# A hybrid decoder layer: parity of the weight buffers, x scaled and rounded in one instruction, half-group splits and two load queues at the start

## The chip, the cores and the metric

The kernel runs on one core of one Trainium2 chip. A core has five engines that run side by side: PE (TensorE, the matrix multiplier), DVE (VectorE), ACT (ScalarE), POOL (GpSimd) and SP (SyncE, which here only issues transfers). Sixteen DMA engines carry data between HBM and the on-chip memory. The metric is the device time in microseconds (us); lower is better.

## The reference

One layer with SEQ = 256 rows and D_MODEL = 2048 is computed in float32: a half-step of a gated feed-forward net (SwiGLU, width 5632), a mixer of attention and gated linear attention, a cross-attention, and a second feed-forward half-step.

```python
x = x + 0.5 * swiglu(rms_norm(x, ffn1_norm[l]), ffn1_w_gate[l], ffn1_w_up[l], ffn1_w_down[l])
x = x + hybrid_mixer(rms_norm(x, mix_norm[l]), pos, w_in[l], ...)
x = x + cross_attention(rms_norm(x, xattn_norm[l]), rms_norm(mem, mem_norm[l]), ...)
x = x + 0.5 * swiglu(rms_norm(x, ffn2_norm[l]), ffn2_w_gate[l], ffn2_w_up[l], ffn2_w_down[l])

def swiglu(h, w_gate, w_up, w_down):
    return (jax.nn.silu(h @ w_gate) * (h @ w_up)) @ w_down
```

The gain of a norm multiplies the columns of x before the product; the factor of each row (the reciprocal root of its mean square) is applied behind it, to the result. So the products of the first half-step need only x times gain.

## The kernel before, in words

**Products.** A weight matrix comes in groups: 512 rows of the inner dimension (four slices k of 128) by 512 columns, 1 MB in float32. PE multiplies in a rounded 32-bit form, so each operand is split into a rounded high part and the remainder: ACT writes the high part (`wh`, line 136), DVE subtracts it from the original for the low part (`wl`, line 137; `split`). A product is then three matmuls, high by high, low by high, and high by low (`mm3`, lines 163 to 165). The rows of x stand on the two sides of a tile t (2 x 128 rows), so a group is 4 x 2 x 3 = 24 matmuls. x itself is held transposed and split in the same way (`xTh`, `xTl`, one pair for each 512 columns). `proj` runs one block of 512 columns over its four groups. From the second block of a half-step on, gate and up are made together by a Strassen-like scheme (`strassen`), which needs the sums `fa`, `fb`, `sa`, `sb` of parts of x (`sums_of`, lines 177 to 186); these are made while the first up block runs.

**Buffers.** The loaded float32 group (`raw`) goes to one of two rings of three buffers: `wp`, which lives for the whole kernel, and `FRAW`, which belongs to the pool of a phase (`half1`, `middle`, `half2`). In the two half-steps `load` (line 121) takes the rings in turn: odd loads of a phase go to `FRAW`, even ones to `wp`; in the middle phase all go to `wp`. The pool of `half2` takes the memory of the pool of `middle`, so a first use of its buffers waits until the tiles that lay there have been read. The split parts `wh` and `wl` have rings of three (`ws`).

**Start.** Three groups of the first gate block and three quarters of x are loaded ahead of all else, x and weights in turn, on SP's queue (lines 108 to 117): the first group in slices of k, the other two in halves. Then `first` (line 432) scales x by the gain and splits it: in slices for group 0 (ACT scales in place at line 295, ACT rounds at line 298, DVE subtracts at line 299), and in halves on POOL (line 297), ACT and DVE for the other three groups. Only group 0 is split slice by slice (`fine` in `wgroup`); groups 1 to 3 are split in one piece. Ten matmuls on a constant run on PE before the first real one (line 428).

**Order.** A scheduler orders the instructions of each engine by priorities and by its own simulation of when operands and buffers come free; `later`/`tick` delay some steps by a count of half groups. Each engine then runs its list strictly in order. SP issues loads in one list too: a load that waits for its buffer holds up all loads behind it, and each hardware DMA also waits for the one eight DMAs earlier, since there are eight DMA semaphores.

**Second half-step.** It begins when the cross-attention's output projection is done: x is updated (line 936), its squares are summed (line 304), and `norm_chunk` transposes it on PE (line 315), scales it by the gain (DVE, line 317) and splits it (lines 320 and 321), one column chunk of 512 after the other. Then `proj` takes the first gate block of `ffn2`.

Of the kernel before, what the change touches and what calls it, by code (L numbers as in the profile page):

```python
# [16 lines left out]
P = 128  # L17
# [31 lines left out]
def layer_kernel(ctx: ExitStack, tc: tile.TileContext, A: dict, out: bass.AP):  # L49
# [24 lines left out]
    def FT(tag, bufs, shape, dt, name):  # L74
        return phase["pool"].tile(shape, dt, tag=tag, name=name, bufs=bufs)
# [31 lines left out]
    with tc.high_priority(100000):  # L107
        SY.dma_start(gain, A["gains"])
        for g in range(3):
            raw = wp.tile([P, 4, 512], F32, tag="raw", name="raw")  # L110
            wload.append(raw)
            step = 2 if g else 1
            xr = FT("h", 8, [P, 4, S], F32, "xr")
            xload.append(xr)
            for k in range(0, 4, step):
                SY.dma_start(xr[:, k:k + step], A["xT"][g, :, k:k + step])
                SY.dma_start(raw[:, k:k + step], A["ffn1_w_gate"][0, g, :, k:k + step])
    xs = [con.tile([P, TT, 512], F32, name=f"x{c}") for c in range(NC)]


    def load(W, c, g):

        if wload:
            return wload.pop(0)
        kn, n = W.shape[-2:]
        with tc.high_priority(WPRI):
            phase["loads"] += 1
            if phase["half_step"] and phase["loads"] % 2:
                raw = FT("raw", FRAW, [P, kn, n], F32, "raw")
            else:  # L130
                raw = wp.tile([P, kn, n], F32, tag="raw", name="raw")
            SY.dma_start(raw, W[c, g])
        return raw

    def split(wh, wl, src):
        SC.copy(wh, src)  # L136
        V.tensor_sub(wl, src, wh.bitcast(F32))  # L137

    def split_tiles(kn, n):
        return tuple(ws.tile([P, kn, n], F32R, tag=x, name=x) for x in ("wh", "wl"))  # L140
# [1 line left out]
    def wgroup(W, c, g, fine=None):  # L142

        raw = load(W, c, g)
        n = W.shape[-1]
        kn = W.shape[-2]
        with tc.high_priority(WPRI):
            wh, wl = split_tiles(kn, n)
            for i in range(kn if fine else 1):
                d = slice(i, i + 1) if fine else slice(0, kn)  # L150
                if fine:
                    fine(i)
                split(wh[:, d], wl[:, d], raw[:, d])
        ks = [(kn * g + kk, wh[:, kk], wl[:, kk]) for kk in range(kn)]
        yield ks[:kn // 2]
        yield ks[kn // 2:]
# [98 lines left out]
    def proj(W, c, lhs, groups, fine=None, last=False):  # L255

        n = W.shape[-1]
        acc = [pa.tile([P, n], F32, tag="acc", name="acc") for _ in range(TT)]
        groups = list(groups)
        for i, g in enumerate(groups):  # L260
            if fine and i:
                fine(4 * i)
            if last and i == len(groups) - 1:
                both = [w for half in wgroup(W, c, g) for w in half]
                for t in range(TT):
                    mm3(acc, lhs, both, i == 0, True, (t,))
                break
            for h, half in enumerate(wgroup(W, c, g, fine if i == 0 else None)):
                mm3(acc, lhs, half, i == 0 and h == 0, i == len(groups) - 1 and h == 1)
                tick()  # L270
        return acc
# [8 lines left out]
    def xtiles(c):  # L280
        hi = con.tile([P, 4, S], F32R, name=f"xTh{c}", tag=f"xTh{c}")
        lo = con.tile([P, 4, S], F32R, name=f"xTl{c}", tag=f"xTl{c}")
        xT[c] = (hi, lo)
        return hi, lo
# [6 lines left out]

    def packed(xr, k0, n, hi, lo, g0):

        if n == 1:
            SC.activation(xr[:, 0], xr[:, 0], AF.Copy, scale=gain[:, g0 + k0:g0 + k0 + 1])
        else:
            G.tensor_tensor(xr, xr, gain[:, g0 + k0:g0 + k0 + n].unsqueeze(2).broadcast_to([P, n, S]), op=ALU.mult)
        SC.copy(hi, xr)
        V.tensor_sub(lo, xr, hi.bitcast(F32))

# [45 lines left out]
    def ffn(pre, r, after, fine=None, last=False):  # L346
# [18 lines left out]
        for part in PARTS:  # L365
            for f in part:
# [11 lines left out]
                        sg.append(s)  # L378
                if sums is None:
                    sums = tuple(FT(n, 1, [P, 4, 4, P], F32R, n) for n in ("sh", "sl"))  # L380
                    sums_of(xT[0], xT[1], lambda i: tuple(p[:, 2 * i:2 * i + 2] for p in sums))
                    upv = proj(wu, f, lhs_x, range(4))
                hs = []
                with tc.high_priority(WPRI):
# [44 lines left out]
    ident = con.tile([P, P], F32, name="ident")  # L429
    make_identity(nc, ident)  # L430

    def first(k):
        if k < 4:
            if k == 0:
                xtiles(0)
            hi, lo = xT[0]
            packed(xload[0][:, k:k + 1], k, 1, hi[:, k:k + 1], lo[:, k:k + 1], 0)
            if k == 3:
                xload.pop(0)
        else:  # L440
            with tc.high_priority(WPRI):
                hi, lo = xtiles(k // 4)
                if xload:
                    xr = xload.pop(0)
                else:
                    xr = FT("h", 8, [P, 4, S], F32, "xr")
                    SY.dma_start(xr, A["xT"][k // 4])
                for j in (0, 2):
                    packed(xr[:, j:j + 2], k + j, 2, hi[:, j:j + 2], lo[:, j:j + 2], 0)

    def load_x():
        ss1 = new_ss("ss1")
# [580 lines left out]
```

## Time and profile before

| | |
|---|---|
| time, median of 3 runs | 1958.72 us (1958.36 to 1960.1) |
| profiled execution, its own time | 1957.67 us |
| its span, first to last instruction | 1955.9 us |
| PE busy | 1925.7 us, 98% |
| DVE busy | 1261.5 us, 64% |
| ACT busy | 976.7 us, 50% |
| POOL busy | 98.1 us, 5% |
| DMA, mean | 213 GB/s |
| mean granted TensorE clock | 0.995 |

All durations that are used below come from this one profiled execution; the time outside its span is 1957.67 - 1955.9 = 1.8 us. In the rows of a timeline the first number is the start in us from the span's start, the second the duration, then come engine, line, operation, the tile written and the tiles read, and in brackets how long the engine had stood idle and what ended that. SPq is SP's queue of DMA issues. Successive matmuls overlap in these rows: each is shown at about 0.39 us, while the starts lie 0.227 us apart.

### The profile page before, as it was taken

The numbers are of one execution on the slowest core, as the hardware profiler recorded it, in microseconds if no ns is written. First come the engines' busy times: TensorE is split into PE (matmuls) and PEld (weight loads), VectorE is DVE, ScalarE is ACT, GpSimd is POOL, SyncE is SP. The second block draws the span as 40 slices with busy tenths as digits, with TensorE's granted clock in tenths as the row PEclk, the third lists the DMA queues.
The fourth block names the chain that finished last, engine by engine and source line by source line (L and its number), as shares of the span: only waits on it lengthen the run. The fifth ranks groups of instructions, "written<-read, shape, count | busy, mean of one in ns | idle before, by whom it ended". The sixth has DMA issues, their size and how long they took to land.

```text
span 1955.9 us, 21245 instructions
## 1 busy us (share of the span) xinstructions
PE 1925.7 (98%) x8760; PEld 1586.1 (81%) x8760; DVE 1261.5 (64%) x947; ACT 976.7 (50%) x876; POOL 98.1 (5%) x101
## 2 busy tenths in 40 slices
PE   8999999999999999999999999899999999999999
PEld 6888878888878888778888889788888788887887
DVE  7776467775578655446775555677746777457863
ACT  6555345553356446444566445545534555335642
POOL 2000000000000000012221000000000000000000
PEclk9999999999999999999999999899999999999999
DMA  9677557775567734445456553567755777556771
GB/s 368 234 236 258 191 146 265 273 267 192 173 222 236 281 127 161 153 169 189 172 215 215 185 182 144 204 228 248 253 193 150 258 271 267 211 177 215 237 284 60
DMA packets 63292, 416.13 MB, mean 213 GB/s; under 512 B 7099, under 2 KB 8251, under 8 KB 14428
## 3 DMA queue, kind: packets, MB, share of 16 engines
q1 hardware_dynamic: 56284, 370.74, 49.6%
q0 software_dynamic: 5760, 41.95, 10.4%
q10 hardware_dynamic: 1152, 2.10, 0.3%
q8 instruction: 68, 1.11, 0.2%
q14 instruction: 28, 0.23, 0.0%
HBM read 370.72 MB, written 2.10 MB: 191 GB/s over the span
## 4 chain that ended last, share of the span: by engine, by line
PE 74%; DVE 16%; ACT 6%; issue 4%; DMA 1%; POOL 0%; SPq 0%; ACTq 0%; DVEq 0%
PE acc L164 20%; PE acc L165 20%; PE acc L163 20%; DVE wl L137 10%; ACT wh L136 5%; PE x L194 5%; DVE raw L212 4%; PE acc L194 1%; PE x L165 1%; PE x L164 1%; PE x L163 1%; DVE h L387 1%; PE y L194 1%; DVE acc L238 1%; PE tp L315 0%
## 5 line engine op out<-in xcount | busy, mean ns | idle before, releaser
L137 DVE TENSOR_TENSOR wl<-raw,wh 128x2048 fp32r<-128x2048 f32 (+1 forms) x407 | 919.2, 2278 | 591.8 <-ACT wh L136 589.9
L136 ACT CAST wh<-raw 128x2048 fp32r<-128x2048 f32 (+1 forms) x407 | 762.4, 1898 | 656.2 <-PE acc L165 477.7
L163 PE MATMUL acc<-wh,xTh 128*128 128x512 f32 x1024 | 403.3, 395 | 15.5 <-ACT wh L136 15.5
L164 PE MATMUL acc<-wl,xTh 128*128 128x512 f32 x1024 | 402.9, 393 | 7.1 <-DVE wl L137 7.0
L165 PE MATMUL acc<-wh,xTl 128*128 128x512 f32 x1024 | 400.7, 391 | 0.0
L163 PE MATMUL acc<-wh,hTh 128*128 128x512 f32 x704 | 274.7, 390 | 0.0
L165 PE MATMUL acc<-wh,hTl 128*128 128x512 f32 x704 | 274.0, 389 | 0.0
L164 PE MATMUL acc<-wl,hTh 128*128 128x512 f32 x704 | 273.9, 389 | 0.0
L163 PEld LDWEIGHTS acc<-wh,xTh 128*128 128x128 f32 x1024 | 193.0, 189 | 59.0 <-ACT wh L136 18.6
L164 PEld LDWEIGHTS acc<-wl,xTh 128*128 128x128 f32 x1024 | 193.5, 189 | 55.4 <-DVE wl L137 16.1
L165 PEld LDWEIGHTS acc<-wh,xTl 128*128 128x128 f32 x1024 | 193.4, 189 | 39.8
L165 PEld LDWEIGHTS acc<-wh,hTl 128*128 128x128 f32 x704 | 132.1, 188 | 27.4
L164 PEld LDWEIGHTS acc<-wl,hTh 128*128 128x128 f32 x704 | 132.2, 188 | 27.3
L163 PEld LDWEIGHTS acc<-wh,hTh 128*128 128x128 f32 x704 | 132.2, 188 | 27.1
L216 POOL DMA_DIRECT2D raw<-raw x40 | 34.6, 865 | 1179.2 <-DVE raw L212 966.2
L212 DVE TENSOR_TENSOR raw<-raw 128x2048 f32<-128x2048 f32 x40 | 91.5, 2287 | 0.7
L165 PE MATMUL x<-wh,xTl 128*128 128x512 f32 x160 | 62.3, 389 | 0.0
L164 PE MATMUL x<-wl,xTh 128*128 128x512 f32 x160 | 62.3, 389 | 0.0
L163 PE MATMUL x<-wh,xTh 128*128 128x512 f32 x160 | 62.2, 389 | 0.0
L228 ACT COPY acc<-x 128x512 f32<-128x512 f32 x20 | 11.4, 571 | 95.6 <-PE x L194 95.6
L163 PE MATMUL acc<-wh,mTh 128*128 128x512 f32 x128 | 50.1, 392 | 0.0
L165 PE MATMUL acc<-wh,mTl 128*128 128x512 f32 x128 | 49.8, 389 | 0.0
(302 smaller groups left out, 1945.0 us busy)
## 6 DMA issues: line engine op xcount, KB each, us to landing
raw<-in_ffn_w_up_dram SPq DMA_DIRECT2D x88, 1024.0 KB, 7.0
raw<-in_ffn_w_down_dram SPq DMA_DIRECT2D x88, 1024.0 KB, 5.0
raw<-in_ffn_w_gate_dram SPq DMA_DIRECT2D x85, 1024.0 KB, 7.1
raw<-in_w_in_dram SPq DMA_DIRECT2D x48, 1024.0 KB, 4.8
raw<-raw POOLq DMA_DIRECT2D x40, 1024.0 KB, 6.9
raw<-in_w_out_dram SPq DMA_DIRECT2D x16, 1024.0 KB, 4.8
raw<-in_xattn_w_k_dram SPq DMA_DIRECT2D x4, 1024.0 KB, 5.6
raw<-in_xattn_w_q_dram SPq DMA_DIRECT2D x4, 1024.0 KB, 4.7
```

Of the source, the lines that this page charges most:

```text
L136: SC.copy(wh, src)
L137: V.tensor_sub(wl, src, wh.bitcast(F32))
L163: PE.matmul(acc[t], lh, wh, start=first and i == 0, stop=False, skip_group_check=seeded)
L164: PE.matmul(acc[t], lh, wl, start=False, stop=False, skip_group_check=seeded)
L165: PE.matmul(acc[t], ll, wh, start=False, stop=last and i == len(half) - 1, skip_group_check=seeded)
L194: PE.matmul(acc, lhs(k)[i], w[:, k], start=first, stop=j == 1 and k == 3, skip_group_check=not start)
L212: V.tensor_add(dst, x, y)
L216: G.dma_start(dst, x, accum_op=ALU.add)
L228: SC.copy(c0l, x)
L238: V.tensor_sub(c0r, ys, x)
L387: V.scalar_tensor_tensor(h, upv[t], r[:, t:t + 1], sg[t], op0=ALU.mult, op1=ALU.mult)
```

## The change

Five edits, all in how work is loaded and split:

1. In the half-steps the even loads of a phase go to `FRAW` and the odd ones to `wp`; before it was the other way round. So the first weight load of a half-step goes to the ring that lives for the whole kernel.
2. In the first gate block x is scaled and rounded in one ACT instruction (`activation` with the gain as scale, straight into `xTh`), and DVE makes the remainder from the unscaled x in one instruction ((x times gain) minus `xTh`), slice by slice for all four groups. POOL takes no part, and no scaled float32 x is written.
3. The groups 1 to 3 of that block are split in halves of two slices, each right behind its half of x.
4. The first two weight slices are loaded on ACT's queue, beside x on SP's.
5. The sums of `sums_of` in a half-step are issued after the last split of the gate block (`issue_after`).

```diff
-                SY.dma_start(raw[:, k:k + step], A["ffn1_w_gate"][0, g, :, k:k + step])
+                (SC if g == 0 and k < 2 else SY).dma_start(raw[:, k:k + step], A["ffn1_w_gate"][0, g, :, k:k + step])
...
-            if phase["half_step"] and phase["loads"] % 2:
+            if phase["half_step"] and phase["loads"] % 2 == 0:
                 raw = FT("raw", FRAW, [P, kn, n], F32, "raw")
...
+    last_split = []
+
     def split(wh, wl, src):
         SC.copy(wh, src)
-        V.tensor_sub(wl, src, wh.bitcast(F32))
+        last_split[:] = [V.tensor_sub(wl, src, wh.bitcast(F32)).ins]
...
-            for i in range(kn if fine else 1):
-                d = slice(i, i + 1) if fine else slice(0, kn)
+            step = fine[0] if fine else kn
+            for i in range(0, kn, step):
+                d = slice(i, i + step)
                 if fine:
-                    fine(i)
+                    fine[1](kn * g + i, step)
                 split(wh[:, d], wl[:, d], raw[:, d])
...
-            if fine and i:
-                fine(4 * i)
...
-            for h, half in enumerate(wgroup(W, c, g, fine if i == 0 else None)):
+            for h, half in enumerate(wgroup(W, c, g, (2 if i else 1, fine) if fine else None)):
...
-        if n == 1:
-            SC.activation(xr[:, 0], xr[:, 0], AF.Copy, scale=gain[:, g0 + k0:g0 + k0 + 1])
-        else:
-            G.tensor_tensor(xr, xr, gain[:, g0 + k0:g0 + k0 + n].unsqueeze(2).broadcast_to([P, n, S]), op=ALU.mult)
+        G.tensor_tensor(xr, xr, gain[:, g0 + k0:g0 + k0 + n].unsqueeze(2).broadcast_to([P, n, S]), op=ALU.mult)
...
-                    sums_of(xT[0], xT[1], lambda i: tuple(p[:, 2 * i:2 * i + 2] for p in sums))
+                    with tc.issue_after(last_split[0]):
+                        sums_of(xT[0], xT[1], lambda i: tuple(p[:, 2 * i:2 * i + 2] for p in sums))
...
+    def first(k0, n):
+        g = k0 // 4
+        if k0 % 4 == 0:
+            xtiles(g)
+            if not xload[g:]:
+                xload.append(FT("h", 8, [P, 4, S], F32, "xr"))
+                SY.dma_start(xload[g], A["xT"][g])
+        hi, lo = xT[g]
+        for k in range(k0, k0 + n):
+            x, h, c = xload[g][:, k % 4], hi[:, k % 4], gain[:, k:k + 1]
+            SC.activation(h, x, AF.Copy, scale=c)
+            V.scalar_tensor_tensor(lo[:, k % 4], x, c, h.bitcast(F32), op0=ALU.mult, op1=ALU.subtract)
```

**ACT at the start of the program.** `xr` is the loaded x, `xTh_132`, `xTh_178`, `xTh_214` and `xTh_250` are the high parts of its four quarters (numbered 132, 176, 216, 258 after the change), `raw` and `wh` the loaded group and its high part. Before, from the last slice of group 0 on:

```order
L295 ACTIVATE xr<-xr,gain 128x256
L298 CAST xTh_132<-xr 128x256
L136 CAST wh<-raw 128x512
L298 CAST xTh_178<-xr 128x512 x2
L136 CAST wh<-raw 128x2048
L298 CAST xTh_214<-xr 128x512 x2
L136 CAST wh<-raw 128x2048 x2
L298 CAST xTh_250<-xr 128x512 x2
```

And after the change, at the same place:

```order
L441 ACTIVATE xTh_132<-xr,gain 128x256
L138 CAST wh<-raw 128x512
L441 ACTIVATE xTh_176<-xr,gain 128x256 x2
L138 CAST wh<-raw 128x1024
L441 ACTIVATE xTh_176<-xr,gain 128x256 x2
L138 CAST wh<-raw 128x1024
L441 ACTIVATE xTh_216<-xr,gain 128x256 x2
L138 CAST wh<-raw 128x1024
L441 ACTIVATE xTh_216<-xr,gain 128x256 x2
L138 CAST wh<-raw 128x1024
L441 ACTIVATE xTh_258<-xr,gain 128x256 x4
L138 CAST wh<-raw 128x1024 x2
```

The first half of a group is now split before the second half of x is touched, and the instructions no longer wait for POOL. DVE's list changes in the same way, and the sums `fa` and `fb` now stand behind the low part of group 3 instead of between groups 2 and 3.

**SP at the start of the second half-step.** The gate groups 0 to 3 of `ffn2` are `raw_8597`, `raw_8667`, `raw_8697`, `raw_8727`; the first up groups are 8779, 8809, 8839, 8869. Before, in the order of issue, with what each load waits for (DMAHW: an earlier DMA; DVE, PE: a reader of the buffer):

```order
L132 DMA raw_8667<-in_ffn2_w_gate_dram 128x2048 [waits DMAHW5_49,DVE_49]
L132 DMA raw_8727<-in_ffn2_w_gate_dram 128x2048 [waits DMAHW6_49,DVE_49]
L132 DMA raw_8809<-in_ffn2_w_up_dram 128x2048 [waits DMAHW7_49,DVE_49]
L132 DMA raw_8597<-in_ffn2_w_gate_dram 128x2048 [waits PE_49]
L132 DMA raw_8697<-in_ffn2_w_gate_dram 128x2048
L132 DMA raw_8779<-in_ffn2_w_up_dram 128x2048
```

After the change the gate groups are `raw_8605`, `raw_8675`, `raw_8705`, `raw_8735`, the up groups 8787, 8817, 8847, 8877:

```order
L132 DMA raw_8605<-in_ffn2_w_gate_dram 128x2048 [waits DMAHW5_49,DVE_49]
L132 DMA raw_8705<-in_ffn2_w_gate_dram 128x2048 [waits DMAHW6_49,DVE_49]
L132 DMA raw_8787<-in_ffn2_w_up_dram 128x2048 [waits DMAHW7_49,DVE_49]
L132 DMA raw_8847<-in_ffn2_w_up_dram 128x2048 [waits DMAHW0_49,DVE_49]
L132 DMA raw_8675<-in_ffn2_w_gate_dram 128x2048 [waits PE_49]
L132 DMA raw_8735<-in_ffn2_w_gate_dram 128x2048
L132 DMA raw_8817<-in_ffn2_w_up_dram 128x2048
```

Group 0 was the fourth load issued and is now the first; groups 1 and 3 are now behind an up group that waits for DVE.

**ACT at the same place.** `junk` are the sums of squares of the four chunks x0 to x3, `xTh0` to `xTh3` the high parts of the transposed chunks. Before:

```order
L304 ACTIVATE junk_8465,ss4_8383<-x1_104 128x512
L304 ACTIVATE junk_8467,ss4_8383<-x1_104 128x512
L320 CAST xTh0_8491<-xg_8498 128x4x128
...
L320 CAST xTh2_8615<-xg_8622 128x4x128
L320 CAST xTh2_8615<-xg_8631 128x4x128
L320 CAST xTh3_8635<-xg_8642 128x4x128
L136 CAST wh_8599<-raw_8597 128x2048
L136 CAST wh_8669<-raw_8667 128x2048
L136 CAST wh_8699<-raw_8697 128x2048
L320 CAST xTh3_8635<-xg_8651 128x4x128
L136 CAST wh_8729<-raw_8727 128x2048
```

After:

```order
L302 ACTIVATE junk_8473,ss4_8391<-x1_104 128x512
L138 CAST wh_8607<-raw_8605 128x2048
L302 ACTIVATE junk_8475,ss4_8391<-x1_104 128x512
L318 CAST xTh0_8499<-xg_8506 128x4x128
...
L318 CAST xTh2_8623<-xg_8630 128x4x128
L318 CAST xTh2_8623<-xg_8639 128x4x128
L138 CAST wh_8677<-raw_8675 128x2048
L138 CAST wh_8707<-raw_8705 128x2048
L138 CAST wh_8737<-raw_8735 128x2048
L318 CAST xTh3_8643<-xg_8650 128x4x128
```

The high part of group 0 has moved ahead of twelve instructions; group 1 now stands where group 0 stood. PE's list follows: the first twelve matmuls of the gate block now stand before the transposes of x2 and x3 (line 315), the other twelve of group 0 behind them, and then group 1. Apart from these places and a few neighbours within the first gate and up blocks of the two half-steps, PE, ACT and DVE keep their order.

More of the change, by code (lines that the diff above doesn't have):

```diff
@@ L430, in layer_kernel @@
     make_identity(nc, ident)
[L432 to L449, printed above, removed]
+    def first(k0, n):
[10 more added lines that the diff above has]
+            V.scalar_tensor_tensor(lo[:, k % 4], x, c, h.bitcast(F32), op0=ALU.mult, op1=ALU.subtract)
     def load_x():
```

## The prediction

> **What bounds the kernel now.** I read the page first (busy shares), then the table of 50 us windows, then PE's waits, then the timeline of the two places that these pointed to.
>
> ```profile
> PE 1925.7 (98%) x8760; PEld 1586.1 (81%) x8760; DVE 1261.5 (64%) x947; ACT 976.7 (50%) x876; POOL 98.1 (5%) x101
> 0.00:50.00 50.00, 42.81 (x172) 33.88 (x173) 34.94 (x30) 31.07 (x42) 9.78 (x15) 0.93 0.94 367
> 250.00:300.00 50.00, 47.56 (x209) 38.64 (x208) 34.56 (x20) 21.73 (x14) 1.70 (x2) 1.00 0.56 172
> 1200.00:1250.00 50.00, 43.38 (x206) 36.14 (x205) 33.35 (x41) 24.83 (x37) 0.70 (x1) 0.90 0.50 189
> 1500.00:1550.00 50.00, 48.48 (x217) 39.53 (x216) 36.63 (x22) 26.44 (x18) 1.71 (x2) 1.00 0.68 223
> PE acc L163 <- ACT wh L136: 15.5, 8, 4.6
> PE acc L164 <- DVE wl L137: 7.0, 17, 2.1
> ```
>
> In a window row the columns behind the length are busy us (and instructions) of PE, PEld, DVE, ACT and POOL, then the granted clock, the DMA share and GB/s. PE is the bound: it lacks 1955.9 - 1925.7 = 30.2 us. Of these 7.2 lie in the first 50 us and 6.6 in 1200 to 1250, where the clock was below 1 as well; the other windows lack 0 to 2.4. The waits name the cause, the two split instructions. So a microsecond saved on PE in one of these two places is saved at the end, as long as no load becomes late behind it.
>
> **Place 1, the start, as it was.**
>
> ```profile
> 13.37 0.39 PE L165 MATMUL acc<-wh,xTl 128*128 128x512 f32 x1
> 16.52 1.22 PE L163 MATMUL acc<-wh,xTh 128*128 128x512 f32 x2 [2.76 <-ACT wh L136]
> 22.85 0.61 PE L163 MATMUL acc<-wh,xTh 128*128 128x512 f32 x1
> 23.28 0.42 PE L164 MATMUL acc<-wl,xTh 128*128 128x512 f32 x1
> 37.36 0.39 PE L163 MATMUL acc<-wh,xTh 128*128 128x512 f32 x1
> 0.00:23.20 23.20, 11.38 (x34) 0.86 0.89 329
> 23.20:37.00 13.80, 13.80 (x62) 1.00 1.03 424
> 18.00:20.00 2.00, 0.30 (x1) 0.30 (x2) 2.00 (x2) 1.95 (x2) 0.00 (x0) 0.50 1.00 416
> ```
>
> Group 0 ends at 13.8; then PE waits for the split of the whole group 1, runs its next matmuls at clock 0.50 (0.43 us apart in the rows at 22.85 and 23.28), and is steady behind that. The gate block's 96 matmuls (34 and 62, the two window rows for PE's work on `acc` alone) end where the 97th starts, at 37.36. The step is (37.36 - 23.28)/62 = 0.227 us.
>
> **What the edits make of it.** Durations of the new forms, and the landings, from these rows:
>
> ```profile
> 3.61 0.51 ACT L295 ACTIVATE xr<-xr,gain 128x256 f32<-128x256 f32 x1 [1.37 <-DMA xr<-in_xT_dram]
> 4.14 0.40 ACT L298 CAST xTh<-xr 128x256 fp32r<-128x256 f32 x1
> 4.58 0.43 DVE L299 TENSOR_TENSOR xTl<-xr,xTh 128x256 fp32r<-128x256 f32 x1 [3.58 <-ACT xTh L298]
> 35.17 1.04 ACT L136 CAST sh<-sa 128x1024 fp32r<-128x1024 f32 x1
> 37.16 1.21 DVE L137 TENSOR_TENSOR sl<-sa,sh 128x1024 fp32r<-128x1024 f32 x1
> 16.50 3.15 DVE L137 TENSOR_TENSOR wl<-raw,wh 128x2048 fp32r<-128x2048 f32 x1 [0.37 <-ACT wh L136]
> 26.94 2.28 DVE L137 TENSOR_TENSOR wl<-raw,wh 128x2048 fp32r<-128x2048 f32 x1
> 16.46 1.04 POOL L297 TENSOR_TENSOR xr<-xr,gain 128x512 f32<-128x512 f32 x1 [0.88 <-DMA xr<-in_xT_dram]
> 11.99 0.33 SPq L447 DMA_DIRECT2D xr<-in_xT_dram  x1
> 13.85 0.38 SPq L455 DMA_DIRECT2D x<-in_x_dram  x1
> 20.18 1.90 ACT L136 CAST wh<-raw 128x2048 fp32r<-128x2048 f32 x1 [0.23 <-DMA raw<-in_ffn_w_gate_dram]
> ```
>
> *One ACT instruction for scale and round:* 0.51 us instead of 0.51 + 0.40 a slice. DVE's new three-operand form isn't in the trace at this shape; I take the 0.43 of the plain one, which is the nearest row; at double, the upper bound, it would cost DVE 0.43 a slice more, 1.7 us a group, which the next sum can bear in all but its last group. A group then costs ACT 4 x 0.51 + 2 x 1.04 = 4.1 us and DVE 4 x 0.43 + 2 x 1.21 = 4.1 us, under PE's 24 x 0.227 = 5.45. *POOL out:* a DVE subtraction beside POOL took 3.15 us, alone 2.28; that goes too.
>
> *Halves:* PE can run from the first half of group 1 on. SP's issue at 11.99 waited for the first weight half of group 1, the one at 13.85 for the second (the eighth DMA before each), so these are the landings. With them unchanged: high part 12.0 + 1.04, low part until 14.25. Two matmuls run on the high part alone, the other 70 follow without a gap if the later halves are in time: the second half is split by 13.85 + 2.25 = 16.1 against a need at 14.25 + 10 x 0.227 = 16.5, and group 3, which landed at 20.2, by 20.2 + 1.04 + 2 x 1.21 = 23.7 against 14.25 + 46 x 0.227 = 24.7. So the 97th matmul starts at 14.25 + 70 x 0.227 = 30.1: 7.2 us earlier.
>
> *Two queues:* the first weight slice is issued 0.9 us earlier (at SP's first issue instead of its third), and all later loads move up by two issues.
>
> ```profile
> 1.65 0.42 SPq L117 DMA_DIRECT2D raw<-in_ffn_w_gate_dram  x1
> 2.00:4.00 2.00, 2.00 (x12) 2.00 (x11) 0.00 (x0) 0.62 (x3) 0.00 (x0) 1.00 0.63 159
> 6.00:8.00 2.00, 1.69 (x5) 0.82 (x5) 1.12 (x2) 1.07 (x4) 0.00 (x0) 1.00 0.91 312
> ```
>
> From 2 to 4 us the DMA engines were busy 0.63 at 159 GB/s, later 0.91 at 312, so there was room for some 0.3 MB, a microsecond of transfer. ACT pays with two issues of 0.42 us ahead of its table load; the 1.37 us that it then waited for x hides them. If all landings come 0.9 us earlier, the gain is 8.1; if none does, 7.2. I take 7.6. [...] The 0.91 and 1.03 shares above agree with a saturated stretch, the 0.63 doesn't.
>
> *Sums later:* fa and fb (1.21 us each) go behind group 3's low part, and the first up group's low part (2.28) behind them: 23.7 + 2.42 + 2.28 = 28.4 against a need at 30.1. If group 3 lands 2 us later than this, PE stalls by the excess; up to 1 us stays in the range.
>
> *Loads behind:* group 3's load now needs the buffer of group 0, split by about 11.9; but its DMA semaphore holds it until 12.0 anyway. What the earlier PE needs next is covered:
>
> ```profile
> 37.64 0.43 SPq L455 DMA_DIRECT2D x<-in_x_dram  x1
> 52.00:54.00 2.00, 2.00 (x11) 1.65 (x10) 1.97 (x2) 0.00 (x0) 0.00 (x0) 1.00 0.00 0
> 56.93 0.62 ACT L304 ACTIVATE junk<-x 128x512 f32<-128x512 f32 x1
> ```
>
> The last x chunk was issued 19 us before its use, and at 52 the DMA engines had nothing to do. Its issue waits for buffers that PE's progress frees, so it moves with PE.
>
> **Place 2, the second half-step.**
>
> ```profile
> 1219.97 1.91 PE L315 MATMUL tp<-ident,x 128*128 128x128 f32 x16
> 1229.91 1.91 PE L315 MATMUL tp<-ident,x 128*128 128x128 f32 x16
> 1234.43 5.49 ACT L136 CAST wh<-raw 128x2048 fp32r<-128x2048 f32 x3
> 1236.37 1.22 PE L163 MATMUL acc<-wh,xTh 128*128 128x512 f32 x2 [4.55 <-ACT wh L136]
> 1237.33 6.68 DVE L137 TENSOR_TENSOR wl<-raw,wh 128x2048 fp32r<-128x2048 f32 x3
> 1252.83 0.39 PE L163 MATMUL acc<-wh,xTh 128*128 128x512 f32 x1
> 1200.38 9.06 SPq L132 DMA_DIRECT2D raw<-in_ffn_w_gate_dram  x2
> 1219.41 0.91 SPq L132 DMA_DIRECT2D raw<-in_ffn_w_gate_dram  x2
> ```
>
> Group 0 was among the loads issued at 1219.41, and its split stood behind the transposes. PE idled 4.55 us, and after two matmuls (until 1236.37 + 1.22 = 1237.6) again until the low part was there (1237.33 + 6.68/3 = 1239.6), then ran for a while at a lowered clock (0.90 in the mean of the window above); the 49th matmul (group 2) started at 1252.83. After the change group 0 takes the load slot of 1200.38, nineteen us before; its split can begin when its `wh` buffer is free, that is when PE has left the next to last block of 12 matmuls before the transposes of x0: 1219.97 - 12 x 0.227 = 1217.2, and ends 1.83 + 2.28 later, at 1221.3 or little more. DVE then starts on x0 at most 1.4 us late (its transposes start at 1219.97), and x0 is needed only at 1229.9. So from 1229.91 on PE runs 12 matmuls, the transposes (1.9) and 12 matmuls: 24 x 0.227 + 1.9 = 7.3, until 1237.2.
>
> Group 1 then waits like group 0 before, but from transposes that start 12 x 0.227 = 2.7 us later, without `fa` (1.2) on DVE and one cast (0.6) on ACT ahead of it (the rows for 128x1024 and 128x512 above): cast at 1234.43 + 2.7 - 1.8 = 1235.3, low part from 1237.2 to 1239.5. Two matmuls go on the high part, then PE idles 1.8 us, and 22 more lead to the 49th at 1239.5 + 5.0 = 1244.5. That is 8.3 us earlier. Groups 2 and 3 are split every 2.3 us after, against PE's 5.4.
>
> **The same elsewhere.** The parity swap alternates two rings of equal size, so later blocks see the same distances; the half-steps before had opposite parities already (half-step 1 an offset of five loads, half-step 2 of eight), and their windows at a part's start read 47.56 and 48.48, 0.9 apart. I take 0, bounds -1 to +1.
>
> **The sum.** 7.6 + 8.3 = 15.9. Against the profiled execution's own 1957.67 us (span 1955.9 and 1.8 around it) that is 1941.8; that execution lies 1.05 under the median 1958.72, so the time forecast is 1942.8 us.
>
> **Rivals.**
>
> *The clock falls once more.* In place 1 or 2 the new short idles (1.2 and 1.8 us) fall so that a stretch runs at 0.50. Price: matmuls 0.43 instead of 0.227 apart; a stretch of 3.4 us, half of the 6.8 from 16.5 to 23.28, loses 1.7 us, two of them 3.4: 1944.5 to 1946.2. Against: the 47.56 window holds a wait of 2.4 us at clock 1.00. [...] But 2.8 us with two matmuls behind them also led to 0.50 here. Chance 0.11.
>
> *Group 1 of the second half-step is late.* Its load now stands behind an up load that waits for group 0's split (about 1221.3 instead of 1219.4). At 1 MB in 2.5 us it lands by 1227 to 1231, needed at 1235.3. If it is over 4 us later, a stall of up to the old 4.55 takes the place of the removed one: 1947. Chance 0.06.
>
> *The start doesn't get faster:* the stream of loads is the bound, group 3 lands after 24 and PE follows it. Then 3 us are left there: 1947.4. Against: at 424 GB/s the 6.3 MB of x and gate groups are through by 20. Chance 0.04.
>
> *Slower than before.* With the swapped rings each Strassen block could wait for its third load, as may happen in the window from 250, which lacks 2.4 us. There are 20 such blocks; from 15.9/20 = 0.8 us each the gain is eaten, and at 1.1 us each the time is 1965. Against it, both offsets ran before, and cost at most those 2.4 and 1.5 us at a part's start. Chance 0.02.
>
> **How the numbers follow.** Forecast 0.77, rivals 0.11, 0.06, 0.04, 0.02. Upper bound of the gains: 8.1 + 10 (no idle at group 1) = 18.1, hence 1940.6; low end of the main case 6.2 + 7.3 = 13.5, hence 1945.2. With the first rival and part of the second and third the range is 1940.0 to 1947.4. A measurement of this kernel tells about 0.2%, 3.9 us, from no change. Faster 0.95, same 0.03, slower 0.02.
>
> **What would show it.** The 97th matmul at 29.3 to 31 instead of 37.36, no POOL work before 50, clock 1.00 in all windows; PE's idle in 1229 to 1245 down from 6.5 (4.55 and the 2.0 behind it) to about 2, and the 49th matmul of the second half-step 8 us earlier against the transposes' start; group 0's load first in its batch. Wrong would be: a window at 0.50, a first up group that PE waits for, or new waits on `raw` in the Strassen blocks.

## The result and the profile after

The changed kernel takes 1941.38 us (median of 4 runs, 1941.36 to 1941.47) against 1959.18 us before (4 runs, 1958.36 to 1960.1): ratio 0.9909, 95% interval 0.9892 to 0.9926. The forecast was 1942.8 us with a range of 1940.0 to 1947.4. The profiled execution took 1941.39 us with a span of 1939.6 us, 16.3 us less than the profiled execution before.

First the busy times and four windows of 50 us of the changed kernel, then PE's waits, in the columns that the prediction used:

```profile
PE 1920.4 (99%) x8760; PEld 1584.2 (82%) x8760; DVE 1258.6 (65%) x956; ACT 976.4 (50%) x881; POOL 88.6 (5%) x95
0.00:50.00 50.00, 47.85 (x203) 39.77 (x204) 36.69 (x41) 33.54 (x49) 1.88 (x10) 1.00 0.96 378
250.00:300.00 50.00, 48.53 (x214) 39.48 (x213) 33.83 (x19) 23.79 (x15) 1.72 (x2) 1.00 0.66 220
1200.00:1250.00 50.00, 48.41 (x231) 40.11 (x230) 39.95 (x43) 29.23 (x38) 0.70 (x1) 1.00 0.60 228
PE acc L166 <- ACT wh L138: 7.2, 5, 1.6
PE acc L167 <- DVE wl L139: 4.3, 15, 1.6
```

PE now lacks 19.2 us of its span instead of 30.2. The first 50 us lack 2.2 instead of 7.2, the window from 1200 lacks 1.6 instead of 6.6. PE's busy time fell too, by 5.3 us: a matmul at the lowered clock counts as busy for longer (0.63 us in the rows of the kernel before at place 2, against 0.39).

The timeline of the start, PE and then ACT:

```profile
6.79 1.22 PE L166 MATMUL acc<-wh,xTh 128*128 128x512 f32 x2 [1.10 <-ACT wh L138]
13.89 0.61 PE L166 MATMUL acc<-wh,xTh 128*128 128x512 f32 x2
14.37 0.50 PE L167 MATMUL acc<-wl,xTh 128*128 128x512 f32 x1
30.38 0.62 PE L166 MATMUL acc<-wh,xTh 128*128 128x512 f32 x2
5.72 0.51 ACT L441 ACTIVATE xTh<-xr,gain 128x256 fp32r<-128x256 f32 x1 [2.56 <-DMA xr<-in_xT_dram]
12.01 1.05 ACT L138 CAST wh<-raw 128x1024 fp32r<-128x1024 f32 x1 [1.16 <-DMA raw<-in_ffn_w_gate_dram]
14.11 1.05 ACT L138 CAST wh<-raw 128x1024 fp32r<-128x1024 f32 x1 [0.24 <-DMA raw<-in_ffn_w_gate_dram]
```

Group 1 starts at 13.89, its third matmul, the first that needs the low part, at 14.37, and 70 matmuls later the 97th at 30.38: 6.98 us earlier than before (37.36). ACT's casts show the landings of group 1's halves, since each ended a wait for a DMA: 12.0 and 14.1 us, where before they were 12.0 and 13.85.

Place 2, the timeline of all engines:

```profile
1192.44 0.33 SPq L132 DMA_DIRECT2D raw<-in_ffn_w_gate_dram  x1
1211.82 2.29 DVE L139 TENSOR_TENSOR wl<-raw,wh 128x2048 fp32r<-128x2048 f32 x1
1224.69 1.91 PE L313 MATMUL tp<-ident,x 128*128 128x128 f32 x16
1227.18 5.51 ACT L138 CAST wh<-raw 128x2048 fp32r<-128x2048 f32 x3
1229.19 0.68 PE L166 MATMUL acc<-wh,xTh 128*128 128x512 f32 x2
1229.12 6.69 DVE L139 TENSOR_TENSOR wl<-raw,wh 128x2048 fp32r<-128x2048 f32 x3
1231.46 0.50 PE L167 MATMUL acc<-wl,xTh 128*128 128x512 f32 x1 [1.59 <-DVE wl L139]
1236.60 0.39 PE L166 MATMUL acc<-wh,xTh 128*128 128x512 f32 x1
```

Group 0's load is the first of its batch, issued at 1192.44 (the slot of 1200.38 before, 7.94 us earlier); its low part is ready at 1214.1, and twelve matmuls run ahead of the transposes at 1224.69. The 4.55 us wait is gone; what is left is 1.59 us for the low part of group 1. The 49th matmul of the block starts at 1236.60.

A third place had not been forecast. Behind the first Strassen block of the second part of the first half-step PE waits for a split; before and after:

```profile
293.95 0.73 PE L163 MATMUL acc<-wh,xTh 128*128 128x512 f32 x2 [2.44 <-ACT wh L136]
286.02 0.73 PE L166 MATMUL acc<-wh,xTh 128*128 128x512 f32 x2 [1.47 <-ACT wh L138]
```

Three landmarks on PE divide the whole difference: the first matmul of the first Strassen block, the matmul of the two rows above (called "the wait at 290"), and the first matmul of the first Strassen block of the second half-step. All numbers are starts in us, read from the timelines.

| kernel | timed, median | profiled, own time | first Strassen block | wait at 290: ends | second half-step's Strassen block | from the wait at 290 to there |
|---|---|---|---|---|---|---|
| before | 1959.18 | 1957.67 | 59.12 | 293.95 (2.44) | 1285.47 | 991.52 |
| changed | 1941.38 | 1941.39 | 52.14 | 286.02 (1.47) | 1269.23 | 983.21 |
| difference | -17.8 | -16.28 | -6.98 | -7.93 | -16.24 | -8.31 |

So in this pair of executions 6.98 us come from the start, 0.95 from the wait at 290, 8.31 from place 2, and nothing that counts from anywhere else. The start's share depends on the pair: against the two other profiles with the old start (first Strassen block at 59.80 and 59.74) it is 7.66 and 7.60.

### The profile page after: what moved, and what is told of

Read it like the earlier page. It is cut to its first block, busy times and chain, and to the rows that moved or that the text cites. A ratio compares the mean times of both kernels' runs of the same rounds, so it can differ in the third digit from the quotient of the medians.

```text
span 1939.6 us, 21252 instructions
## 1 busy us (share of the span) xinstructions
PE 1920.4 (99%) x8760; PEld 1584.2 (82%) x8760; DVE 1258.6 (65%) x956; ACT 976.4 (50%) x881; POOL 88.6 (5%) x95
## 3 DMA queue, kind: packets, MB, share of 16 engines
q8 instruction: 68, 1.11, 0.2%
## 4 chain that ended last, share of the span: by engine, by line
PE 73%; DVE 16%; ACT 6%; issue 4%; POOL 0%; DMA 0%; ACTq 0%; SPq 0%; DVEq 0%
PE acc L167 20%; PE acc L168 20%; PE acc L166 20%; DVE wl L139 11%; ACT wh L138 5%; PE x L197 4%; DVE raw L215 4%; PE x L167 1%; PE x L168 1%; PE x L166 1%; PE acc L197 1%; DVE acc L241 1%; DVE h L386 1%; PE y L197 1%; PE tp L313 0%
## 5 line engine op out<-in xcount | busy, mean ns | idle before, releaser
L139 DVE TENSOR_TENSOR wl<-raw,wh 128x2048 fp32r<-128x2048 f32 (+2 forms) x410 | 917.5, 2258 | 578.3 <-ACT wh L138 577.5
L138 ACT CAST wh<-raw 128x2048 fp32r<-128x2048 f32 (+2 forms) x410 | 762.9, 1886 | 646.2 <-PE acc L168 463.4
```

Of the source, the lines that this page charges most:

```text
L139: last_split[:] = [V.tensor_sub(wl, src, wh.bitcast(F32)).ins]
```

## The experiments

Times in brackets behind a median are its lowest and highest run. Kernels of one job are compared with runs of the kernel before in that job (medians 1957.4 to 1958.9 us). The changed kernel was timed in the first job only (1941.38 beside 1959.18), so differences of some tenths against it are read from the profiles.

### Each half of the change alone

The kernel before with the parity alone:

```diff
-            if phase["half_step"] and phase["loads"] % 2:
+            if phase["half_step"] and phase["loads"] % 2 == 0:
```

> The kernel before with the first edit alone (even loads of a half-step go to the phase's ring). My theory: the two places are independent, and the parity alone earns place 2. The 49th matmul of the second half-step's first gate block comes 14.6 us behind the start of the block instead of 22.9, the start stays as it was (97th matmul at 37.4), and the profiled execution's time is 1957.7 - 8.3 = 1949.4 us (1948.2 to 1950.6). Rival: the 0.95 us that the changed kernel also gained at 290 us (a shorter wait for a split behind the first Strassen block of the second part) belongs to the parity: then 1948.4, and the wait there is 1.5 instead of 2.4 us. Other rival: place 2 needs the edit that issues the sums after the last split; then group 1 waits longer by the two sums on DVE, 2.4 us, and the time is 1951.8.

Measured: 1950.39 us (1949.33 to 1952.16), ratio 0.9962 (0.9949 to 0.9976). The changed kernel with the old parity, that is the same two lines the other way round:

> The changed kernel with the old parity. My theory: the start alone earns 7.0 us (97th matmul at 30.4 instead of 37.4), place 2 has its old waits of 4.6 and 2.0 us and its low clock: 1957.7 - 7.0 = 1950.7 us (1949.5 to 1952). Rival: the 0.95 us at 290 us belongs to the start, since loads are issued at other times: 1949.7. The gains of this kernel and of the parity alone should add up to the 16.3 us of the profiled executions, within about 1 us.

Measured: 1949.28 us (1948.91 to 1950.27), ratio 0.9956 (0.9943 to 0.9968). Rows of PE, two from the parity alone, then two from the start alone:

```profile
294.60 0.73 PE L163 MATMUL acc<-wh,xTh 128*128 128x512 f32 x2 [2.42 <-ACT wh L136]
1240.26 0.50 PE L164 MATMUL acc<-wl,xTh 128*128 128x512 f32 x1 [1.54 <-DVE wl L137]
286.04 0.73 PE L166 MATMUL acc<-wh,xTh 128*128 128x512 f32 x2 [1.49 <-ACT wh L138]
1229.47 1.22 PE L166 MATMUL acc<-wh,xTh 128*128 128x512 f32 x2 [5.41 <-ACT wh L138]
```

The two gains add up, within the spread of the runs: 8.4 and 9.5 us against the kernel before of that job (1958.81), together 17.9, where both edits at once gave 17.8 in their own job. The parity alone turns the wait of place 2 into the same 1.5 us; the stretch from the wait at 290 to the second half-step's Strassen block takes 983.4 us, 8.1 less than before. The start alone puts the first Strassen block at 52.10 (7.02 earlier), keeps a long wait at place 2, and has the short wait at 290: the 0.95 us belong to the start's edits, against my first expectation. Its place 2 was by chance 1.2 us shorter than before (990.3), because only 5 matmuls stood 0.43 us apart behind the wait instead of 11.

### The kernel before, once more

> The kernel before once more, for a second profiled execution. The first one lies at 1957.67 us, its timed runs between 1958.36 and 1960.1, while the changed kernel's runs agree within 0.1 us. My theory: the spread comes from the two places, where the lowered clock lasts longer or shorter, and from single late transfers such as the one of 0.95 us at 290 us. Expected: a time of 1956.5 to 1960, the same waits of 4.6 and 2.0 us, with the stretches of 0.43 us between matmuls of another length than 6.8 us behind 16.5 and about 7 behind 1237. Rival: the spread lies elsewhere (Strassen blocks): then the shifts against the first profile are spread over the span.

Measured: 1959.23 us (1957.02 to 1960.77), profiled at 1959.99, that is 2.3 us over the first profile. Place 2 has the same waits of 4.55 and 2.07 us. At the start group 0 ended earlier, so the waits behind it are longer (4.43 and 1.10 instead of 2.76 and 1.96), but group 1's first low part was used 0.21 us earlier; what makes this execution longer is the clock behind the waits. Its rows at the start and at 290:

```profile
17.16 1.22 PE L163 MATMUL acc<-wh,xTh 128*128 128x512 f32 x2 [4.43 <-ACT wh L136]
19.49 0.80 PE L164 MATMUL acc<-wl,xTh 128*128 128x512 f32 x1 [1.10 <-DVE wl L137]
294.66 1.22 PE L163 MATMUL acc<-wh,xTh 128*128 128x512 f32 x2 [2.42 <-ACT wh L136]
```

Behind the start's waits 11 matmuls stood 0.43 us apart instead of 7 (the first Strassen block at 59.80 instead of 59.12), and behind the wait at 290 five more did, which cost 1.5 us; in the first profile none did. So nearly all of the 2.3 us between these two executions sits behind long waits. That the whole spread of the kernel before, some 4 us, does so is not shown. The changed kernel's four runs lie within 0.11 us, but its variants with one queue and with 12 constant matmuls (below) spread over 2.2 and 1.9 us.

### The start, part by part

The changed kernel with groups 1 to 3 split in one piece:

```diff
-            for h, half in enumerate(wgroup(W, c, g, (2 if i else 1, fine) if fine else None)):
+            for h, half in enumerate(wgroup(W, c, g, (4 if i else 1, fine) if fine else None)):
```

> The changed kernel with the groups 1 to 3 of the first gate block split in one piece each. My theory: the halves carry most of the start's gain. Group 1's cast waits for its second half (14.1): high part at 16.0, low part at 18.3, third matmul of group 1 at 18.3 instead of 14.4, so 3.9 us later and 1945.3 us if the clock stays; with the lowered clock behind the two idles, for as long as in the kernel before (6.8 us), up to 3.4 more, 1948.7. Rival: the gain came from taking POOL and one ACT instruction a slice out of the way, so that whole groups would be in time: within 1 us of 1941.4.

Measured: 1947.77 us (1947.05 to 1948.21), 6.4 over the changed kernel. ACT's cast of group 1 and what PE waited for:

```profile
14.23 1.90 ACT L138 CAST wh<-raw 128x2048 fp32r<-128x2048 f32 x1 [0.38 <-DMA raw<-in_ffn_w_gate_dram]
16.19 1.22 PE L166 MATMUL acc<-wh,xTh 128*128 128x512 f32 x2 [3.45 <-ACT wh L138]
18.51 0.79 PE L167 MATMUL acc<-wl,xTh 128*128 128x512 f32 x1 [1.11 <-DVE wl L139]
```

The cast starts when the second half has landed, and PE's third matmul of group 1 starts at 18.51 instead of 14.37: 4.14 us, 3.9 expected. A slow stretch behind it (8 matmuls 0.43 us apart) makes the rest of the 6.1 us by which the first Strassen block is late (58.22). The halves carry nearly all of the start's gain.

Two ACT instructions a slice instead of one:

```diff
-            SC.activation(h, x, AF.Copy, scale=c)
-            V.scalar_tensor_tensor(lo[:, k % 4], x, c, h.bitcast(F32), op0=ALU.mult, op1=ALU.subtract)
+            SC.activation(x, x, AF.Copy, scale=c)
+            SC.copy(h, x)
+            V.tensor_sub(lo[:, k % 4], x, h.bitcast(F32))
```

> The changed kernel with x scaled in place and then rounded by a second ACT instruction, slice by slice on ACT (no POOL). My theory: the fusion earns 0.41 us a slice on ACT, but ACT had idle time ahead of group 1 (0.45 + 1.16 us), so only what is behind that counts: the second half of group 1 is late by about 0.5 us, and groups 2 and 3 keep pace (2.75 us of ACT a half against PE's 2.72): the 97th matmul at 30.9 to 31.4, time 1941.9 to 1942.4 us. Rival: the fusion carries the start's gain, 16 slices by 0.41 us on a full ACT: 6.5 us, 1948.

Measured: 1941.8 us (1941.72 to 1941.98), 0.4 over the changed kernel; the first Strassen block starts at 52.30, 0.16 late. The fused instruction is worth next to nothing here, because ACT has idle time ahead of group 1.

All first loads on SP's queue:

```diff
-                (SC if g == 0 and k < 2 else SY).dma_start(raw[:, k:k + step], A["ffn1_w_gate"][0, g, :, k:k + step])
+                SY.dma_start(raw[:, k:k + step], A["ffn1_w_gate"][0, g, :, k:k + step])
```

> The changed kernel with all first loads on SP's queue. My theory: from the landing of group 1's first half (12.0 us, the same before and after) the start is bound by the transfers, so the second queue earns nothing: x's first slice lands about 1 us earlier than with two queues, the first matmul starts at 6.1 to 6.3 instead of 6.8, the 97th still at 30.1 to 30.7, and the time is 1941.1 to 1941.8 us. Rival, as in the forecast's term of 8.1: the issue was the bound, all landings come 0.9 us later, the 97th at 31.3 and the time 1942.3.

Measured: 1942.19 us (1941.67 to 1943.9); the profiled run is the 1943.9. Its rows:

```profile
3.61 0.51 ACT L441 ACTIVATE xTh<-xr,gain 128x256 fp32r<-128x256 f32 x1 [1.38 <-DMA xr<-in_xT_dram]
12.47 1.04 ACT L138 CAST wh<-raw 128x1024 fp32r<-128x1024 f32 x1 [1.05 <-DMA raw<-in_ffn_w_gate_dram]
6.11 0.73 PE L166 MATMUL acc<-wh,xTh 128*128 128x512 f32 x2 [0.88 <-ACT wh L138]
13.57 0.73 PE L166 MATMUL acc<-wh,xTh 128*128 128x512 f32 x2 [1.11 <-ACT wh L138]
14.82 0.79 PE L167 MATMUL acc<-wl,xTh 128*128 128x512 f32 x1 [0.53 <-DVE wl L139]
```

x's first slice is there 2.1 us earlier than with two queues (3.61 against 5.72), and group 0 starts earlier. Group 1's first half is cast at 12.47, 0.46 us later than in the changed kernel. But this landing moves by itself: SP's issue that waits for it came at 11.99, 12.53, 12.63 and 12.86 in the four executions with one queue (three of them with the old start) and between 11.45 and 12.66 in the nine with two, in the mean 12.50 and 12.14. That is a shift of some tenths, within the spread; nine tenths are not seen. (That the issue marks the landing is read from the traces before and after the change: in each, 396 hardware DMAs take eight semaphores in turn, 104 of them wait for their own, which the DMA eight before counted up, and this issue starts 0.02 and 0.08 us behind the last count of that half, at 11.97 and 11.99.) PE comes to group 1 earlier, waits 1.11 and 0.53 us, uses the low part at 14.82, 0.45 late, and then runs six matmuls slowly (15.41 to 17.98). So of the 2.0 us by which the first Strassen block is late (54.17), 0.45 come from the landing and 1.6 from the slow stretch. The median is 0.8 us over the changed kernel's, the lowest run 0.3. Whether the second queue earns more than the luck of the clock stays open.

The sums of x not tied to the last split:

```diff
-                    with tc.issue_after(last_split[0]):
+                    if True:
```

> The changed kernel without the rule that issues the sums after the last split of the gate block. My theory: at the start the sums fb and sa then stand ahead of group 3's low halves, which come 1.0 us later (25.0 instead of 24.0) and are needed at 25.4, so nothing is lost. At place 2 fa, fb and sa (3.1 us) stand ahead of the transposes' scaling on DVE, which has 2.1 us of idle time there: PE's wait for group 1 grows by 0.4 to 1.9 us. Time 1941.8 to 1943.3 us. Rival: both places lose the whole of two sums, 2.4 us each: 1946.2; or neither loses: 1941.4.

Measured: 1942.5 us (1942.31 to 1942.63), 1.1 over the changed kernel. The sum was met, the places were wrong. ACT's cast of group 1 at the start, and PE's waits at the start and at place 2:

```profile
12.56 1.05 ACT L138 CAST wh<-raw 128x1024 fp32r<-128x1024 f32 x1 [1.70 <-DMA raw<-in_ffn_w_gate_dram]
26.43 0.50 PE L167 MATMUL acc<-wl,xTh 128*128 128x512 f32 x1 [0.33 <-DVE wl L139]
1232.65 0.50 PE L167 MATMUL acc<-wl,xTh 128*128 128x512 f32 x1 [1.56 <-DVE wl L139]
```

At place 2 the sums fit into DVE's idle time and the wait stays at 1.56. At the start the first Strassen block is 1.22 us late: some 0.55 because group 1 landed late in this execution (12.56), most of the rest because group 3's low part stands behind two sums, `fb` and `sa`, and PE waits for it there (0.33 us, and 0.10 us more since the next matmul starts 0.33 instead of 0.227 us behind). So the rule is worth 0.7 us in this execution, at the start.

### What was left: two waits taken away

The changed kernel with the second load of the second half-step in the long-lived ring too, and the third in the phase's (the phase is marked with 2 instead of True):

```diff
-            if phase["half_step"] and phase["loads"] % 2 == 0:
+            if phase["half_step"] and (phase["loads"] % 2 == 0 if phase["half_step"] == 1 or phase["loads"] > 4 else phase["loads"] > 2):
...
-    open_phase("half2", True)
+    open_phase("half2", 2)
```

> The changed kernel, with the first two loads of the second half-step both in the ring that lives for the whole kernel (loads 3 and 4 in the phase's ring, then alternating as before). My theory: what is left at place 2, 1.59 us of waiting for the low part of group 1, comes from the split of group 1 standing behind the transposes' casts; with its load in the long-lived ring the split stands two instructions of x earlier on ACT and DVE, the wait is gone and the time is 1941.4 - 1.6 = 1939.8 us. Rival: DVE, which now makes the low part (2.3 us) before the last update of x, delays x2's and x3's transposes, and PE waits there instead: 1941.0 to 1942.5.

Measured: 1939.89 us (1939.88 to 1940.4), 1.5 less than the changed kernel. ACT's cast of group 1, DVE's low part, and the window:

```profile
1220.38 1.90 ACT L138 CAST wh<-raw 128x2048 fp32r<-128x2048 f32 x1
1222.31 2.29 DVE L139 TENSOR_TENSOR wl<-raw,wh 128x2048 fp32r<-128x2048 f32 x1
1200.00:1250.00 50.00, 50.00 (x239) 41.95 (x238) 40.97 (x44) 29.78 (x38) 0.69 (x1) 1.00 0.60 232
```

PE is busy through the whole window. The wait for group 1 was the order of its split on ACT and DVE, which followed from the ring of its load.

On that kernel, group 1 of the first block split in slices as group 0 is; and, on the changed kernel and on this one, 12 instead of 10 matmuls on a constant:

```diff
-            for h, half in enumerate(wgroup(W, c, g, (2 if i else 1, fine) if fine else None)):
+            for h, half in enumerate(wgroup(W, c, g, (2 if i > 1 else 1, fine) if fine else None)):
```

```diff
-WARM = 10
+WARM = 12
```

> The changed kernel with 12 instead of 10 of the matmuls on a constant ahead of the first real one, so that PE is busy until about 6.6 us and its idle of 1.1 us ahead of the first real matmul is gone. In the profiled execution of the changed kernel the matmuls from 6.8 to 9.9 stood 0.43 us apart. My theory: that slow stretch costs nothing, since PE must have group 1's low part to go on (14.3 us) whether group 0 ends at 12.3 or 13.9: with 12 matmuls group 0 runs at 0.227 us and ends at 12.3 to 12.6, PE waits 0.5 to 1.1 us for group 1, the 97th matmul starts at 30.1 to 30.7, time 1941.1 to 1941.8 us. Rival: the slow stretch costs its 1.5 us: 1939.9. Other rival: PE's new waits ahead of group 1 bring a slow stretch there, as with one queue: up to 1.5 us more, 1942.9.

> The kernel with the first two loads of the second half-step in the long-lived ring (1939.9 us), and group 1 of the first block split slice by slice as group 0 is. My theory: the start is bound by group 1's first half, which lands at 12.0; a cast of one slice (0.60) and its low part (0.69) end 1.0 us earlier than those of a half (1.05 and 1.22), so PE can go on with the low part at 13.3 instead of 14.3: 1938.9 us where group 0 has run at full step (ends at 12.3), and 1939.5 to 1939.9 where it ran slowly and ends at 13.9. Rival: ACT and DVE take longer for eight slices than for four halves (0.15 us a half on each), and the second half or group 2 become late: 1940 to 1940.5.

> Both of the edits above together on the same kernel. My theory: with group 0 at full step and group 1's low part at 13.3 the 97th matmul starts at 29.1 to 29.6 and the time is 1938.7 to 1939.2 us; the two edits are worth more together than alone, since each takes away one of the two things that PE waits for ahead of group 1. Rival: the waits ahead of group 1 (about 0.5 and 0.4 us) bring a slow stretch: 1940 to 1940.5.

Measured, beside a kernel before of 1958.89 us: 12 matmuls on the changed kernel 1942.67 us (1941.44 to 1943.31); the slices 1939.15 (1938.38 to 1939.81); both 1939.02 (1938.95 to 1939.45), ratio to the kernel before 0.9901 (0.9887 to 0.9916). Rows of PE: two of the first, one of the second and one of the third.

```profile
7.01 0.73 PE L166 MATMUL acc<-wh,xTh 128*128 128x512 f32 x2 [0.46 <-ACT wh L138]
14.31 0.50 PE L167 MATMUL acc<-wl,xTh 128*128 128x512 f32 x1 [0.52 <-DVE wl L139]
12.94 0.51 PE L167 MATMUL acc<-wl,xTh 128*128 128x512 f32 x1
13.86 0.50 PE L167 MATMUL acc<-wl,xTh 128*128 128x512 f32 x1 [0.23 <-DVE wl L139]
```

With 12 matmuls group 0 ran at full step and ended at 13.05, and yet the first low part of group 1 came at 14.31, as in the changed kernel (14.37), and the profiled time is the same (1941.44): the slow stretch in group 0 had cost nothing. That the two extra matmuls brought the full step is not shown: with ten, group 0 ran at full step in five of the other executions with the new start, and at the slow step in three. The other runs of it are up to 1.9 us longer, and no trace shows why; a slow stretch behind the 0.5 us wait would do it. The slices move that low part to 12.94 and 13.86. In both it comes 1.40 us behind the start of the cast (11.54 and 12.46), against 2.36 with halves (14.37 behind 12.01), so the slices earn 0.96 us here and the rest is the landing; in the median they gained 0.7 us on the kernel that they were added to (1939.89). The kernel with both is the fastest by its median, 2.4 us below the changed kernel; against the one with the slices alone (0.13) that is no difference.

## Why the prediction was right

**Place 1, forecast 7.6 (7.2 to 8.1), measured 6.98, a little under the range of this term.** The mechanism was right: 70 matmuls without a gap behind group 1's first low part, which was forecast for 14.25 if the landings stayed and used at 14.37. The uncertain step is the second queue, of which I took half (0.4 of 0.9 us). In this pair the landing of group 1's first half didn't move (12.0 and 14.1 for the two halves, against 12.0 and 13.85), but the execution before had the earliest such landing of the four with one queue; in the mean over all executions it came 0.36 us earlier with two, about the half that I took, within a spread of a microsecond. So the size of this term stays open. What the queue did to the transfers can be read: the DMA engines were ahead from 4 to 6 us (379 GB/s against 275 before) and behind from 8 to 10 (266 against 353), and over the first 12 us moved 250 against 245; x's first slice, issued at 1.18 us in both, was ready 2.1 us later (5.72 against 3.61). This pair of profiles agrees to 0.2 us with the 7.2 that I had put for landings that don't move; the other two profiles with the old start, which give 7.60 and 7.66, don't decide it.

**The three-operand form on DVE** took 0.48 us a slice (0.43 taken, 0.86 the bound, which was an estimate of mine: twice the 0.43) and didn't matter.

**Place 2, forecast 8.3, measured 8.31.** Each step came where it was put, moved by the 7.94 us gained until then: group 0's load at 1192.44 (1200.38 - 7.94), group 1's cast at 1227.18 (1235.3 - 7.94 = 1227.4), its low part at 1229.12 + 6.69/3 = 1231.35 (1231.6), the wait 1.59 (1.8), the 49th matmul at 1236.60 (1236.6).

**The same elsewhere, forecast 0 (-1 to +1), measured 0.95**, but through the start's edits and not through the parity. If the reading in the last section holds, it is luck: it would hang on where an instruction load happens to fall. No Strassen block waited for its third load, which was the mechanism of the slower rival.

**The clock, a rival at 0.11.** It did not fall in either place: behind the waits there the matmuls stood 0.23 us apart. What I had not priced is that in the start 5 matmuls of group 0 stood 0.43 us apart (why is not shown, see the last section); it cost nothing, since PE would have waited for group 1 anyway.

**The other rivals.** Group 1 of the second half-step wasn't late: its cast at 1227.18 followed the casts of x without waiting for a load. In the start group 3 did land later than I had taken, at 21.6 instead of 20.2, but the low part of its first half was ready at 23.95, and PE used it at 25.39.

**From the profile to the median.** I added the 1.05 us by which the profiled execution before lay below its median. In the changed kernel there is no such offset: profiled time and median agree. The second profile of the kernel before suggests why: there the executions differed by slow stretches behind long waits, and these waits are gone. The offset is the larger part of the 1.4 us by which the forecast was too long; the rest is 16.28 against 15.9. That this sum is so close is in part luck: 0.6 us too much at place 1 and 0.95 that I had not forecast nearly cancel.

## What to carry to other kernels

Where the bound engine idles only at the start of a phase, look for the first load of that phase and for the buffer it must wait for: a buffer that lives longer than the phase lets the load and its split run beside the old phase's work. Where an operand goes through a chain of load, round and subtract, the pieces should be as small as the transfers that bring them; splitting them was worth 6 us here, fusing an instruction on an engine with idle time 0.4. And a long wait on PE may cost more than its length, by a stretch at the lowered clock whose length changes from run to run (7 matmuls 0.43 us apart behind the start's waits in one execution of the kernel before, 11 in the other), so taking the waits away can also make the times steadier, as it did in the changed kernel's own runs (0.11 us from the lowest to the highest, 1.74 before).

## What the runs showed of the hardware

**Slow matmuls where the clock column reads 1.00.** In the profiled execution of the changed kernel the matmuls from 7.8 to 9.9 us stood 0.43 us apart instead of 0.227, and the windows there read 1.00; the second row counts 7 matmuls in 2 us, where 10 to 11 stand in a window at full step. In the kernel with two loads in the long-lived ring (third row) group 0 ran at the same slow step, and there the column reads 0.50:

```profile
6.00:8.00 2.00, 1.21 (x3) 0.98 (x4) 1.72 (x4) 2.00 (x6) 0.00 (x0) 1.00 0.93 314
8.00:10.00 2.00, 2.00 (x7) 1.52 (x6) 2.00 (x5) 1.55 (x5) 0.00 (x0) 1.00 0.88 266
8.00:10.00 2.00, 2.00 (x6) 1.60 (x5) 2.00 (x5) 1.47 (x4) 0.00 (x0) 0.50 0.71 214
```

So the distance of the matmuls' starts, and not the column, tells whether PE ran slowly. The packed traces show what differs: the first record of the clock lies at 10.11 us in the changed kernel's execution and at 6.25 us in that of the kernel before, and ahead of it the column reads 1.00 without a record. So the slow stretch of the changed kernel, whose last slow step leads to 9.94 us, ends where its record begins. Whether the clock had been low since the start of the program there or fell behind the wait of 1.10 us is not shown.

Nor does the idle time ahead tell here whether PE runs slowly behind it: behind the same wait of 2.4 us at 290 five matmuls ran slowly in the second profile of the kernel before and none in the first, and PE went slow behind 1.11 and 0.53 us (one queue) and not behind 1.30 (slices). In the trace of the kernel before, apart from the end of the program, the clock is recorded at 0.50 twice: from 16.49 us for 6.83 us, at the end of the wait of 2.76 us, and from 1235.05 us for 10.24 us, inside the wait of 4.55 us. With one queue PE had no such wait ahead of its slow stretch: from 6.11 to 14.82 us it stood idle for the 1.11 and 0.53 us only, with two matmuls between them, and from 15.41 to 17.98 its starts lay 0.43 us apart.

**An instruction load beside a transfer's last packet.** The wait at 290 was 2.42 to 2.44 us in all three executions with the old start and 1.47 to 1.75 in the ten with the new one. The split there waits for an accumulating transfer that POOL issues: ACT's cast starts 0.10 us behind the landing of its last part both before (290.19) and after the change (282.26). The DMA view of the kernel before, 288 to 289.5 us (queue, packets, MB, share), and of the changed kernel, 281 to 282.5:

```profile
q0 software_dynamic: 32, 0.13, 43.6%
q14 instruction: 1, 0.01, 1.4%
```

```profile
q0 software_dynamic: 32, 0.13, 43.5%
```

In the kernel before an instruction packet of 8 KB runs from 288.93 to 289.26. The transfer's last 8 KB packet ends at 288.95 and the last of its sixteen 4-byte packets starts at 289.25, while the other fifteen start between 288.65 and 288.82; the last part of the completion came 0.95 us behind the others (290.09 against 288.97 to 289.14). In the other two executions with the old start the view from 286 to 291.5 us counts one such instruction packet of q14 too. The changed kernel has 21252 instructions instead of 21245; there the packet runs at 274.06, and all sixteen parts land within 0.2 us (281.98 to 282.16). That is read from the traces; no run moved the instruction load by itself, so that it holds up the last part is my guess and not shown.
